# Encoder layer on one core: 27 instead of 24 in-projection pieces beside the first attention, 35 instead of 38 beside the second

## The chip, the cores and the metric

The kernel runs on one core of one Trainium2 chip, in a single launch. The metric is the device time of one execution in microseconds (us). The engines are named as the profile names them: PE (TensorE, matrix products; PEld is its weight load), DVE (VectorE), ACT (ScalarE), POOL (GpSimd), SP (SyncE, here the queue that issues nearly all DMAs). Every product is made of float32 values split into a high and a low part, as three matmuls (high x high, high x low, low x high).

## The reference

```python
# x (1, 2048, 1024) f32, one layer
h = rms_norm(x, norm_mix)
z = h @ w_in                      # q_A 512 | k_A 128 | v_A 128 | q_B 512 | k_B 512 | v_B 512 | gate_A 1024 | gate_B 1024
y_a = windowed_gqa(q_a, k_a, v_a, sink)      # 8 heads, 2 kv heads, |t-s| <= 128, ALiBi, sink logit
y_b = neighborhood_attn(q_b, k_b, v_b, rpb)  # 8 heads, 8 x 16 neighbourhood on the 32 x 64 grid
gates = sigmoid(concat(g_a, g_b) + b_gate)
merged = gates[:, :1024] * (y_a @ w_proj_a) + gates[:, 1024:] * (y_b @ w_proj_b)
x = x + merged @ w_out
x = x + square(relu(rms_norm(x, norm_mlp) @ w_up)) @ w_down
return rms_norm(x, norm_final)
```

## The kernel before

The 2048 tokens are four blocks of 512. The kernel goes through these stages, most of them one after another on PE:

1. The in-projection of blocks 0 and 1, by a scheme of seven products of half-size blocks (`in_quad`). Its results go to scratch tensors in HBM: `qs_a`, `ks_a`, `vs_a` for the first attention, `qs_b`, `ks_b`, `vs_b` for the second, `zg` for the gates.
2. The first attention (A): 32 units `attn_a(g, i)`, one for each of two key heads and 16 blocks of 128 queries. Beside it runs a part of the plain in-projection of blocks 2 and 3.
3. The second attention (B): 32 units `attn_b`, one for each of 8 heads and 4 column strips of the grid. Beside it runs another part of the plain in-projection.
4. What is left of the plain in-projection, then gates, projections, `w_out`, and the two products of the feed-forward part.

**A plain piece** is one 128-column tile of the in-projection for one block: `feature_tile` (L203 to L205), 8 x 3 matmuls of 128x512 into a PSUM bank `mm`, from the weight tile `whl` and the normalised input `hT`. There are 34 column tiles (`dense`: one of k_A, one of v_A, four of q_A, then k_B, q_B, v_B four times, then 16 of the gates), each for blocks 2 and 3, so 68 pieces. With each tile go its weight load on SP (L190), the split of the weights on ACT (L179) and POOL or DVE (L180), and with each piece its eviction and store. The generator `chain(dense)` hands them out one by one, in that order; each step loads the tile after next and splits the next.

**A unit of A** has, on PE, eight score matmuls `s` (L792), three groups of four transposes `pt` (L810, two PSUM banks) and six products `av` with the values (L815 with the high part, L816 with the low part of the transposed weights). DVE adds the bias and takes the maximum from PSUM (L794, four times), adds and inverts the sums (L800, L801), makes the low part of each transposed group (`pl`, L814) and adds the result's halves (L822). ACT takes the exponentials (L799, four times) and the high parts (`ph`, L813). POOL scales by the inverse sums (L803). A unit at the edge (i = 0 or 15) has two groups of transposes. **A unit of B** is built alike: scores L955, maximum L960, exponentials L966, transposes L983, high and low parts L988 and L989, products L995.

**The order** of the instructions on each engine is made when the program is built, by a scheduler that times the program and puts what is ready first; it follows the program's order in priority. `drive` lets the units of an attention go ahead of their second halves by two. `paced` then feeds the pieces in: piece n of a stage is held behind the last product of unit n x 32 // total - lag, so that the pieces are spread over the stage:

```python
def paced(filler, pieces, total, lag):
    for n in pieces:
        at = min(n * 32 // total - lag, 31)
        with tc.issue_after(done[at]) if at >= 0 else nullcontext():
            next(filler, None)
```

Here `done` is the list of the last products of the units of that attention (emptied between A and B), and `total` the number of pieces that the 32 units are to be spread over. For A the calls stand in two parts, one ahead of the later halves of the keys and values (`load_kv`), one behind; for B too, one after the first 15 units and one at the end, ahead of stage 4. `chain` is one generator, so a piece that A takes is one that B does not.

Of the kernel before, what the change touches and what calls it, by code (L numbers as in the profile page):

```python
# [95 lines left out]
def encoder_layer(ctx, tc, x, norm_mix, w_in, b_gate, sink, rpb, w_pa, w_pb, w_out,  # L96
# [77 lines left out]
    def flush(keep=0, queue=A):  # L174
        while len(pending) > keep:
            queue.dma_start(*pending.pop(0))
# [650 lines left out]
    def chain(gens):  # L827

        for k, g in enumerate(gens):
            if k + 2 < len(gens):  # L830
                next(gens[k + 2])
            if 0 < k < len(gens) - 1:
                next(gens[k + 1])
            yield from g

    def drive(units, live, last, ahead=2):

        for u in units:
            next(u)
            live.append(u)  # L840
            if len(live) > ahead:
                next(live.pop(0), None)
        while last and live:
            next(live.pop(0), None)
# [7 lines that stand above are left out]
# [26 lines left out]
    fill = chain(dense)  # L878
# [3 lines left out]
    for g in (1, 0):  # L882
        load_kv(g, 0)
    drive((attn_a(g, i) for g in (1, 0) for i in range(7)), live, False)
    paced(fill, range(12), 24, 3)
    flush(queue=SY)
    for g in range(2):
        load_kv(g, 1, began[8 + 3 * g])
    drive((attn_a(g, i) for g in range(2) for i in range(7, 16)), live, True)
    paced(fill, range(12, 24), 24, 3)  # L890
    del done[:]
    flush(queue=SY)
    s_a.close()
# [133 lines left out]

    units = ahead_of(all_b(), 1)
    drive((next(units) for _ in range(15)), live, False)
    paced(fill, range(20), 38, 4)  # L1030
    flush(queue=SY)
    drive(units, live, True)
    flush(queue=SY)
# [27 lines left out]

    first_y = load_y(0)
    first_load = last_dma[0]
    paced(fill, range(20, 44), 38, 4)
    s_h.close()


# [596 lines left out]
```

## Time and profile before

| | us |
|---|---|
| median of 3 runs | 2603.46 (2603.23 to 2605.39) |
| the profiled execution | 2603.09 |
| its span, first to last instruction | 2601.3 |
| first attention with its pieces, from the first score matmul to the first of B | 362.5 to 608.5 |
| second attention, to its last score matmuls | 608.5 to 978 |

The span is a little shorter than the execution's own time, which has what lies around the program too. Busy times of an engine are sums over its instructions. A matmul is drawn from its start to the end of its flow through the array, so that consecutive ones overlap in the drawing: the distance from one start to the next is what a matmul takes of PE. "Idle before" is the time in which the engine did nothing ahead of an instruction, with the instruction that released it.

### The profile page before, as it was taken

Reading aid. Unit: us, or ns where it says so; the run is one execution under the profiler, and the core shown is the slowest. Engines: PE = TensorE matmul, PEld = TensorE weight load, DVE = VectorE, ACT = ScalarE, POOL = GpSimd, SP = SyncE. Lnnn points to the kernel's source line nnn. Section 1 sums busy time; section 2 is a strip of 40 time slices with the busy share of each in tenths; the row PEclk is TensorE's granted clock in tenths of the full one; section 3 lists DMA queues with packets and bytes.
Section 4 is the critical chain, followed back from the end, with each engine's and each line's share of the span. In section 5 each row is a group of like instructions: output and inputs, shape, how many; then the busy total and the mean of one; then the engine's idle time right before and its main releaser. Section 6 shows DMA issues by size and latency. Waiting matters only on the chain.

```text
span 2601.3 us, 34630 instructions
## 1 busy us (share of the span) xinstructions
PE 2570.3 (99%) x12140; PEld 2143.2 (82%) x12140; DVE 1608.5 (62%) x2621; ACT 1232.9 (47%) x2261; POOL 366.8 (14%) x493
## 2 busy tenths in 40 slices
PE   8999999999999999999999999999999999999999
PEld 6888788788888888888888888888888888888887
DVE  8866666665544444665478667766656534554766
ACT  5334356665655555542335544644454322323454
POOL 1000124444645531000000000100000000000010
PEclk9999999999999999999999999999999999999999
DMA  5657485465976746865466665844428825444555
GB/s 186 203 154 207 135 260 160 121 170 154 244 211 180 205 137 189 270 205 160 144 195 213 232 227 202 307 167 149 155 102 314 288 97 186 146 149 167 186 191 173
DMA packets 354128, 490.40 MB, mean 189 GB/s; under 512 B 28809, under 2 KB 188809, under 8 KB 351777
## 3 DMA queue, kind: packets, MB, share of 16 engines
q1 hardware_dynamic: 346896, 471.14, 57.2%
q10 hardware_dynamic: 7056, 17.04, 1.8%
q8 instruction: 96, 1.57, 0.3%
q14 instruction: 80, 0.65, 0.1%
HBM read 328.64 MB, written 159.45 MB: 188 GB/s over the span
## 4 chain that ended last, share of the span: by engine, by line
PE 92%; DVE 3%; DMA 2%; ACT 2%; issue 1%; SPq 0%; POOL 0%; POOLq 0%; ACTq 0%; DVEq 0%
PE b L302 16%; PE b L304 16%; PE b L303 16%; PE mm L203 6%; PE mm L205 6%; PE mm L204 6%; PE zb L302 3%; PE zb L304 3%; PE zb L303 3%; PE pt L203 2%; PE pt L204 2%; PE pt L205 2%; PE av L995 2%; PE pt L983 2%; PE s L955 2%; PE pt L810 1%
## 5 line engine op out<-in xcount | busy, mean ns | idle before, releaser
L303 PE MATMUL b<-dwh,dah 128*128 128x512 f32 x896 | 348.5, 389 | 0.0
L304 PE MATMUL b<-dwh,dah 128*128 128x512 f32 x896 | 347.6, 389 | 0.0
L302 PE MATMUL b<-dwh,dah 128*128 128x512 f32 x896 | 339.6, 389 | 0.0
L298 ACT CAST dah<-da 128x1024 fp32r<-128x1024 f32 (+1 forms) x128 | 120.9, 945 | 367.9 <-PE b L304 245.4
L299 DVE TENSOR_TENSOR dah<-da,dah 128x1024 fp32r<-128x1024 f32 (+1 forms) x128 | 139.7, 1091 | 224.5 <-ACT dah L298 221.3
L303 PE MATMUL b<-ubh,uwhlb 128*128 128x512 f32 x592 | 230.3, 389 | 0.0
L302 PE MATMUL b<-ubh,uwhlb 128*128 128x512 f32 x592 | 230.2, 389 | 0.0
L304 PE MATMUL b<-ubh,uwhlb 128*128 128x512 f32 x592 | 229.2, 389 | 0.0
L203 PE MATMUL mm<-hT,whl 128*128 128x512 f32 x544 | 218.6, 402 | 0.0
L205 PE MATMUL mm<-hT,whl 128*128 128x512 f32 x544 | 215.3, 396 | 0.0
L204 PE MATMUL mm<-hT,whl 128*128 128x512 f32 x544 | 214.4, 394 | 0.0
L303 PEld LDWEIGHTS b<-dwh,dah 128*128 128x128 f32 x896 | 168.2, 188 | 35.0
L302 PEld LDWEIGHTS b<-dwh,dah 128*128 128x128 f32 x896 | 168.2, 188 | 34.9
L304 PEld LDWEIGHTS b<-dwh,dah 128*128 128x128 f32 x896 | 168.2, 188 | 34.9
L302 PE MATMUL zb<-zh,zwhl 128*128 128x512 f32 x476 | 186.0, 393 | 6.9 <-DVE st L242 2.0
L303 PE MATMUL zb<-zh,zwhl 128*128 128x512 f32 x476 | 185.8, 390 | 0.0
L304 PE MATMUL zb<-zh,zwhl 128*128 128x512 f32 x476 | 183.0, 390 | 1.8 <-DVE zwhl L299 1.8
L293 DVE TENSOR_TENSOR uc<-b,uc 128x512 f32<-128x512 f32 x160 | 109.2, 689 | 103.9 <-PE b L304 103.0
L1534 POOL TENSOR_TENSOR st<-st,power 128x1 f32<-128x1 f32 x16 | 13.3, 841 | 925.1 <-DVE st L1533 925.0
L302 PEld LDWEIGHTS b<-ubh,uwhlb 128*128 128x128 f32 x592 | 111.1, 188 | 23.5 <-issue 0.4
L303 PEld LDWEIGHTS b<-ubh,uwhlb 128*128 128x128 f32 x592 | 111.1, 188 | 23.1
L304 PEld LDWEIGHTS b<-ubh,uwhlb 128*128 128x128 f32 x592 | 111.1, 188 | 23.0
(255 smaller groups left out, 5842.2 us busy)
## 6 DMA issues: line engine op xcount, KB each, us to landing
at<-uc SPq DMA_DIRECT2D x224, 256.0 KB
da<-at SPq DMA_DIRECT2D x96, 512.0 KB
dw<-in_w_down_dram SPq DMA_DIRECT2D x160, 256.0 KB
uraw<-in_w_up_dram SPq DMA_DIRECT2D x32, 1024.0 KB
raw<-in_w_in_dram SPq DMA_DIRECT2D x34, 512.0 KB
zraw<-in_w_in_dram SPq DMA_DIRECT2D x16, 1024.0 KB
z<-zg SPq DMA_DIRECT2D x64, 256.0 KB
zg<-zc SPq DMA_DIRECT2D x32, 256.0 KB
```

What stands on the lines that cost most here:

```text
L203: PE.matmul(ps, lh, rh, start=first, stop=False)
L204: PE.matmul(ps, lh, rl, start=False, stop=False)
L205: PE.matmul(ps, ll, rh, start=False, stop=last)
L293: return eng.tensor_tensor(out=out, in0=a, in1=b, op=op).ins
L298: casts.append(A.copy(hi, src).ins)
L299: return eng.tensor_tensor(out=lo, in0=src, in1=hi.bitcast(F32), op=ALU.subtract).ins
L302: PE.matmul(ps, lh, rh, start=first, stop=False, skip_group_check=True)
L303: PE.matmul(ps, lh, rl, start=False, stop=False, skip_group_check=True)
L304: PE.matmul(ps, ll, rh, start=False, stop=last, skip_group_check=True)
L955: PE.matmul(ps[:, :n], q[:, i, :], kv[:, z, B_R0[i] // 4 : (B_R0[i] + B_NR[i]) // 4, 4 * B_C0[j] : 4 * (B_C0[j] + w)], start=z == 0, stop= ...
L983: PE.transpose(pt[:kp, at + (i - i0) * P : at + (i - i0 + 1) * P], s[i][:, rr : rr + kp], ident)
L995: last = PE.matmul(po[:, i0 * P : (i0 + ni) * P], v[:kp, c, :], src[:kp, o : o + ni * P], start=first, stop=(c == 7 and z == 1), skip_grou ...
```

## The change

The pieces beside A become 27 instead of 24: 13 in the first part, 14 in the second, spread as 27 over the 32 units, with the lag of 3 as before. Of B's pieces the first part becomes 18 instead of 20, the second 23 instead of 24, spread as 35 over the units instead of 38, with the lag of 4 as before. The three pieces that go over to A are both blocks of the third k_B tile and the first block of the third q_B tile.

```diff
@@ -882,12 +882,12 @@
     for g in (1, 0):
         load_kv(g, 0)
     drive((attn_a(g, i) for g in (1, 0) for i in range(7)), live, False)
-    paced(fill, range(12), 24, 3)
+    paced(fill, range(13), 27, 3)
     flush(queue=SY)
     for g in range(2):
         load_kv(g, 1, began[8 + 3 * g])
     drive((attn_a(g, i) for g in range(2) for i in range(7, 16)), live, True)
-    paced(fill, range(12, 24), 24, 3)
+    paced(fill, range(13, 27), 27, 3)
     del done[:]
     flush(queue=SY)
     s_a.close()
@@ -1027,7 +1027,7 @@
     units = ahead_of(all_b(), 1)
     drive((next(units) for _ in range(15)), live, False)
-    paced(fill, range(20), 38, 4)
+    paced(fill, range(18), 35, 4)
     flush(queue=SY)
     drive(units, live, True)
     flush(queue=SY)
@@ -1061,7 +1061,7 @@
     first_y = load_y(0)
     first_load = last_dma[0]
-    paced(fill, range(20, 44), 38, 4)
+    paced(fill, range(18, 41), 35, 4)
     s_h.close()
```

The order that this gives is built anew for every engine from the middle of A to the end of B.

## The prediction

> **What bounds the kernel now.** I read the page first, then the windows by stage, then PE's own groups and time line inside the first attention.
>
> ```profile
> span 2601.3 us, 34630 instructions
> PE 2570.3 (99%) x12140; PEld 2143.2 (82%) x12140; DVE 1608.5 (62%) x2621; ACT 1232.9 (47%) x2261; POOL 366.8 (14%) x493
> PEclk9999999999999999999999999999999999999999
> PE 92%; DVE 3%; DMA 2%; ACT 2%; issue 1%; SPq 0%; POOL 0%; POOLq 0%; ACTq 0%; DVEq 0%
> ```
>
> TensorE (PE) is the chain that ends last, at full granted clock throughout. The change leaves the number of its matmuls as it is: 68 plain pieces of 72 matmuls stand before and after, only at other places. So the time can move only through the time in which PE stands still between instructions. The windows by stage say where that is: first attention with its pieces (362.5 to 608.5), second attention (608.5 to 978), its last units and the pieces left over (to 1026).
>
> ```profile
> core 0: us, PE busy (x) PEld busy (x) DVE busy (x) ACT busy (x) POOL busy (x), PEclk, DMA share, GB/s
> 362.50:608.50 246.00, 240.40 (x1300) 199.93 (x1299) 152.16 (x448) 162.91 (x466) 110.70 (x173) 1.00 0.60 165
> 608.50:978.00 369.50, 368.95 (x2128) 322.81 (x2127) 179.20 (x456) 209.27 (x503) 191.92 (x213) 1.00 0.69 190
> 978.00:1026.00 48.00, 47.27 (x259) 40.15 (x259) 17.90 (x34) 25.36 (x48) 7.02 (x7) 1.00 0.46 131
> ```
>
> PE is idle 5.60 us in the first attention, 0.55 us in the second, though the second is half as long again. The donor stage is full and the receiving stage has holes. The holes are not spread evenly:
>
> ```profile
> 362.50:392.00 29.50, 28.75 (x158) 23.90 (x157) 17.63 (x66) 18.24 (x64) 13.46 (x24) 1.00 0.92 273
> 417.00:425.00 8.00, 7.50 (x48) 6.04 (x47) 6.49 (x18) 7.67 (x23) 5.08 (x7) 1.00 0.62 167
> 425.00:451.00 26.00, 26.00 (x141) 22.00 (x140) 15.06 (x44) 15.27 (x43) 10.47 (x17) 1.00 0.44 115
> 480.00:492.00 12.00, 9.91 (x61) 7.95 (x60) 9.00 (x27) 8.71 (x23) 5.64 (x8) 1.00 0.49 127
> 584.00:592.00 8.00, 7.63 (x45) 5.93 (x44) 5.43 (x18) 7.48 (x25) 5.57 (x8) 1.00 0.79 234
> ```
>
> Between two holes PE is 26.00 of 26.00 us busy; the holes come every 33 us or so, four units apart (32 units in 246 us, 7.7 us each). The pacing rule says why. Piece n of the first attention may start behind unit n*32//24 - 3, which for n = 3 to 23 gives 1,2,3, 5,6,7, 9,10,11, 13,14,15, 17,18,19, 21,22,23, 25,26,27: units 0, 4, 8, 12, 16, 20 and 24 free no piece, and there PE has attention alone.
>
> **What one hole costs.** The time line of PE from the last piece before one hole to the first piece behind it (start, length, line, tile, count):
>
> ```profile
> 584.19 0.39 PE L815 MATMUL av<-ph,va 128*128 128x512 f32 x1
> 584.42 0.69 PE L792 MATMUL s<-ka,qa 128*128 128x288 f32 x4
> 584.95 0.39 PE L816 MATMUL av<-pl,va 128*128 128x512 f32 x1
> 585.18 1.03 PE L810 MATMUL pt<-ident,sa 128*128 128x128 f32 x8
> 585.97 1.68 PE L792 MATMUL s<-ka,qa 128*128 128x288 f32 x6
> 587.64 0.50 PE L815 MATMUL av<-ph,va 128*128 128x512 f32 x1
> 587.99 0.39 PE L816 MATMUL av<-pl,va 128*128 128x512 f32 x1
> 588.22 0.83 PE L792 MATMUL s<-ka,qa 128*128 128x288 f32 x4
> 588.89 0.42 PE L815 MATMUL av<-ph,va 128*128 128x512 f32 x1
> 589.54 0.50 PE L816 MATMUL av<-pl,va 128*128 128x512 f32 x1 [0.23 <-DVE pl L814]
> 589.87 0.39 PE L815 MATMUL av<-ph,va 128*128 128x512 f32 x1
> 590.11 0.60 PE L810 MATMUL pt<-ident,sa 128*128 128x128 f32 x4
> 590.46 0.48 PE L816 MATMUL av<-pl,va 128*128 128x512 f32 x1
> 590.78 0.60 PE L810 MATMUL pt<-ident,sa 128*128 128x128 f32 x4
> 591.13 0.48 PE L203 MATMUL mm<-hT,whl 128*128 128x512 f32 x1
> ```
>
> The steps from start to start are PE's real prices: a 512-wide matmul 0.23 us (584.95 to 585.18), a 288-wide one 0.53/4 = 0.13 us (584.42 to 584.95), a transpose 0.11 us (590.11 to 590.78 holds four and one 512-wide matmul: (0.67 - 0.23)/4). From 584.19 to 591.13 stand 8 wide matmuls, 14 of 288 and 16 transposes: 1.84 + 1.86 + 1.76 = 5.46 us of work in 6.94 us. **The hole costs 1.5 us**, while the window shows only 8.00 - 7.63 = 0.37 us idle, since a matmul's drawn length (0.39) is longer than its step. [...] Priced by busy time alone, a hole would be worth 0.4 us and the whole change some 3 us.
>
> The same count over the whole stage checks the price:
>
> ```profile
> L203 PE MATMUL mm<-hT,whl 128*128 128x512 f32 x180 | 72.3, 401 | 0.0
> L810 PE MATMUL pt<-ident,sa 128*128 128x128 f32 x328 | 50.1, 272 | 2.5 <-DVE pl L814 2.3 <-DVE sta L801 0.2
> L792 PE MATMUL s<-ka,qa 128*128 128x288 f32 x224 | 46.3, 313 | 0.8 <-DVE sta L794 0.5
> L815 PE MATMUL av<-ph,va 128*128 128x512 f32 x80 | 33.3, 416 | 0.3 <-DVE ya L822 0.3
> L816 PE MATMUL av<-pl,va 128*128 128x512 f32 x80 | 33.3, 416 | 1.9 <-DVE pl L814 1.4
> ```
>
> L204 and L205 have 180 as well, so 700 wide matmuls x 0.23 = 161.0, 328 transposes x 0.11 = 36.1, 224 x 0.1325 = 29.7, and 48 small ones left of the 1300 at about 0.1 = 4.8: 231.6 us of work in 246, so 14.4 us lost (the rounding of 0.23 makes this good to 1.5 us either way). One part is a single accident, at 485.2 to 487.5:
>
> ```profile
> 486.29 0.16 DVE L800 TENSOR_TENSOR sta<-sta 128x4 f32<-128x4 f32 x1 [1.93 <-ACT sa L799]
> 486.76 0.69 DVE L814 TENSOR_TENSOR pl<-pt,ph 128x512 fp32r<-128x512 f32 x1
> 487.51 0.66 PE L810 MATMUL pt<-ident,sa 128*128 128x128 f32 x4 [2.02 <-DVE pl L814]
> ```
>
> VectorE (DVE) sits 1.93 us in L800, waiting for ScalarE's four exponentials of a later unit; the split L814 is queued behind it, and PE's next transposes wait for the PSUM bank that L814 frees: 2.02 us. The other 12.4 us over seven regular holes and one small one near 600 us are 1.55 us each, as counted above.
>
> The cause of a regular hole is VectorE. A unit needs of it four reductions, three splits and one addition:
>
> ```profile
> L814 DVE TENSOR_TENSOR pl<-pt,ph 128x512 fp32r<-128x512 f32 x81 | 55.3, 688 | 9.1 <-ACT ph L813 8.6
> L794 DVE CUSTOM_DVE_ANT_0 sa<-s,biasa,byhead 128x288 f32<-128x288 f32 x112 | 53.7, 513 | 32.5 <-PE s L792 18.1 <-PE pt L810 14.3
> L822 DVE TENSOR_TENSOR ya<-av,ya 64x512 f32<-64x512 f32 x27 | 18.4, 680 | 6.6 <-ACT ya L821 6.5
> ```
>
> 4 x 0.513 + 3 x 0.688 + 0.680 = 4.8 us, against PE's 8 x 0.13 + 12 x 0.11 + 6 x 0.23 = 3.7 us. Alone, a unit runs at VectorE's pace and PE loses about 1.1 us plus the latency of the first split; with a piece (24 x 0.23 = 5.5 us more on PE) PE is the slower of the two and loses nothing.
>
> **The change part by part.**
> *First attention, 24 to 27 pieces.* The gates become n*32//27 - 3 = 0,1,2, 4 to 8, 10 to 15, 17 to 21, 23 to 27: units 3, 9, 16 and 22 free no piece, and unit 0 now does. In the built program PE's order follows this: stretches without a piece lie between pieces 5 and 6, 10 and 11, 16 and 17, 21 and 22, where they lay between 2|3, 5|6, 8|9, 11|12, 14|15, 17|18 and 20|21; the one between 2 and 3 is cut in its middle. The stretch 10|11 has, instruction for instruction on PE, the order of the hole timed above, so it costs 1.5 us again. Six regular holes become four: -2 x 1.5 = **-3.0 us** (bounds -1.5 to -4). The accident's place gets a piece; in the new VectorE order the splits that a hole's transposes need stand ahead of that L800 in all four holes, or (16|17) one stands behind it with some 5 us of PE work between by the steps above. I take it as gone: **-2.0 us** (0 to -2.0). The hole at the start (0.75 us idle in 362.5:392, the largest of the regular ones) keeps its first half and has a piece in its second: **-1.3 us** (0 to -2.5).
>
> *What else a piece brings.* Each moved tile of two pieces brings a weight load and two stores per piece on SP's queue, one split on ScalarE and GpSimd, one eviction. In the first attention these engines have room (ACT 162.91, DVE 152.16, POOL 110.70 of 246 us, DMA share 0.60), PE waits there for no DMA, and keys, values and queries of the later half come out of earlier pieces than before, so their loads on SP start no later: 0.
>
> *Second attention, 38 to 35.* The rule n*32//35 - 4 still passes over every unit: each of the 32 frees at least one piece; only three of the six units that freed two lose the second one. A unit with one piece has 5.5 us of filler against the same 1 to 2 us of VectorE surplus. In its second half the kernel before already runs with about one piece per unit, and PE's idle time over the whole stage is 0.55 us. I take **+0.5 us** (0 to +4). The order on PE of the last units and of pieces 62 to 67 is the same, so the 0.73 us idle of 978 to 1026 stays.
>
> *Sum:* -3.0 - 2.0 - 1.3 + 0.5 = **-5.8 us**. The profiled execution took 2603.09 us (its span 2601.3 and 1.8 around it), so 2597.3; the median of the runs, 0.4 us above it, becomes **2597.7 us**. About 0.2% (5.2 us) is what a measurement of this kernel can tell from no change, so this stands just beyond that bound.
>
> **The rivals.**
> *The accident moves on (2600.6 us, chance 0.30).* VectorE's order is written anew, and one of the four holes, or the shortened start, has a split behind a waiting L800 after all: 2.0 us come back, and the start gives 0.4 instead of 1.3. -2.9 us. For it: it happened in one hole of seven. Against: the new order shows no such place without cover.
>
> *The holes close further (2594.9 us, chance 0.13).* With nine pieces in eight units less backlog is left at VectorE when a hole begins, and the four left cost 0.8 us instead of 1.5: 2.8 us more. Against: stretch 10|11 is the old order again.
>
> *The holes are a matter of buffers (2603.5 us, chance 0.05).* Two PSUM banks for transposes, not the missing piece, would make the bubble; then it moves with the units and nothing is gained. [...] The trace speaks against it as the whole cause: with the same two banks the windows with pieces show none (26.00 of 26.00).
>
> *Slower: the second attention starts to starve (2608.7 us, chance 0.07).* With one piece per unit, PE reaches the products av before ScalarE or VectorE has the halves of the transposes:
>
> ```profile
> 857.02 0.39 PE L995 MATMUL av<-phb,vb 128*128 128x256 f32 x1 [0.39 <-ACT phb L988]
> ```
>
> With 0.16 us hidden by the drawn length that is 0.55 us a time. In each of the 20-odd units that now have a single piece and had one or two before, this would be 20 x 0.55 = 11 us, less the first attention's 5.8: +5.2. It decides from about 11 such stalls for no gain at all (11 x 0.55 = 6), from 20 for slower by over 0.2%. Against: with half of the stage already at one piece per unit, its idle time is 0.55 us in all.
>
> **How the numbers follow.** The forecast has 0.45. Its own range, from the bounds of the two holes, the start and the second attention, is 2596 to 2599.5; about three parts in four of it lie beyond 0.2%. With the closing holes, faster by over 0.2% has 0.45 x 0.75 + 0.13 plus a little from milder forms of both, 0.52; slower by over 0.2% takes half of the starving case and some for what no row shows, 0.06; the rest, 0.42, is within 0.2%. The range for 8 in 10 reaches from the closing holes to the moved accident and a little beyond: 2594.5 to 2602.
>
> **What would show it.** Right: PE idle time of the first attention (5.60 us) falls to about 3; the waiting of transposes for L814 (2.3 us) is gone; holes stand at four places some 50 us apart; the first attention is longer by three pieces (3 x 5.5 = 16.6 us) less the gain, the second shorter by as much; PE idle in the second stays under 1.5 us. Wrong: a wait of about 2 us on L814 at a new place (the accident), or idle time of several us at L995 in the second attention (starving), or the same number of holes as before.

## The result, and the profile after

| | before | after |
|---|---|---|
| median of 10 runs, us | 2603.65 (2602.24 to 2605.80) | 2610.30 (2605.60 to 2613.91) |
| ratio, 95% interval | | 1.0024 (1.0016 to 1.0033) |
| the profiled execution, us | 2603.09 | 2611.57 |
| its span, us | 2601.3 | 2609.8 |
| mean granted TensorE clock in it | 1.000 | 0.998 |

The change makes the kernel slower by 6.6 us. The page of after (span; busy time of the engines):

```profile
span 2609.8 us, 34644 instructions
PE 2576.0 (99%) x12140; PEld 2143.9 (82%) x12140; DVE 1609.2 (62%) x2621; ACT 1232.7 (47%) x2261; POOL 366.3 (14%) x493
```

As many matmuls as before, a span 8.5 us longer. The windows of after by stage (first attention A; second attention B to its last score matmuls):

```profile
core 0: us, PE busy (x) PEld busy (x) DVE busy (x) ACT busy (x) POOL busy (x), PEclk, DMA share, GB/s
362.50:624.00 261.50, 256.06 (x1374) 214.12 (x1373) 156.06 (x451) 167.19 (x469) 113.08 (x174) 0.99 0.60 163
624.00:986.00 362.00, 358.49 (x2051) 309.18 (x2050) 176.08 (x453) 205.40 (x500) 189.16 (x212) 1.00 0.69 189
```

PE's idle time in A is 5.44 us (before 5.60; the prediction said about 3), in B 3.51 us (before 0.55; said under 1.5). As in the prediction, busy time hides most of it. So from here on a **stall** is counted from starts: the distance of two starts on PE less the price of the first instruction (0.227 us for 512 wide, 0.132 for 288, 0.110 for a transpose, others by width, an estimate from these), summed over a stage. B is taken to its last product (1015.4 before, 1023.7 after):

| stalls, us | before | after | difference | forecast |
|---|---|---|---|---|
| A | 16.9 | 16.2 | -0.7 | -6.3 |
| B | 12.3 | 21.6 | +9.3 | +0.5 |

The sum, +8.6, is the difference of the spans (8.5) within 0.1 us. The waits of PE in after that have to do with both attentions (engine, line, waited for: total, times, longest):

```profile
PE pt L810 <- DVE pl L814: 2.5, 1, 2.5
PE s L955 <- DMA kb<-ks_b: 2.2, 1, 2.2
PE s L955 <- DVE stb L960: 0.8, 4, 0.3
...
PE av L995 <- ACT phb L988: 0.2, 1, 0.2
```

Three things stand behind the two numbers.

**1. The accident moved.** The time lines of PE, DVE and ACT in A's first hole of after (start, length, and in brackets the idle time before and who ended it):

```profile
413.17 0.77 PE L792 MATMUL s<-ka,qa 128*128 128x288 f32 x4
416.44 0.66 PE L810 MATMUL pt<-ident,sa 128*128 128x128 f32 x4 [2.50 <-DVE pl L814]
417.03 0.75 PE L815 MATMUL av<-ph,va 128*128 128x512 f32 x1
417.58 0.63 PE L816 MATMUL av<-pl,va 128*128 128x512 f32 x1
418.01 0.63 PE L815 MATMUL av<-ph,va 128*128 128x512 f32 x1
```

```profile
413.80 0.16 DVE L800 TENSOR_TENSOR sta<-sta 128x4 f32<-128x4 f32 x1 [2.28 <-ACT sa L799]
...
414.27 0.69 DVE L449 SCALAR_TENSOR_TENSOR z<-mm,z 128x512 fp32r<-128x512 f32 x1
415.69 0.69 DVE L814 TENSOR_TENSOR pl<-pt,ph 128x512 fp32r<-128x512 f32 x1 [0.72 <-ACT ph L813]
```

```profile
413.67 0.57 ACT L448 ACTIVATE z<-mm 128x512 fp32r<-128x512 f32 x1
414.15 1.03 ACT L179 CAST whl<-raw 128x1024 fp32r<-128x1024 f32 x1
415.08 0.57 ACT L813 CAST ph<-pt 128x512 fp32r<-128x512 f32 x1
```

It is the picture of 485.2 before, at a new place: DVE sits 2.28 us in L800 waiting for exponentials, the split L814 is queued behind it, and PE's transposes wait for the bank that L814 frees. L800 is not what ends last, though, here or before. L814 also needs the high part that ACT makes (L813), and on ACT this stands behind the same exponentials. ACT before:

```profile
485.65 0.52 ACT L799 ACTIVATE sa<-sa,sta 128x288 f32<-128x288 f32 x1
...
486.17 0.56 ACT L813 CAST ph<-pt 128x512 fp32r<-128x512 f32 x1
```

Before, L813 ends at 486.73 and L814 starts at 486.76; in after L813 ends at 415.65 and L814 starts at 415.69. With L800 out of the way both would have waited until then. In after an eviction (L448) and a weight cast (L179) stand between the exponentials and L813 and put it off by 1.41 us (413.67 to 415.08); the stall is 2.50 us, not 2.02. And behind the stall matmuls start 0.43 us apart (417.58, 418.01) where 0.23 is the rule: the granted clock is 0.50 from 417.1 on, for 3.41 us.

**2. B waits for the keys of its second head.** PE and the DMA issues of SP in after:

```profile
676.92 0.38 PE L955 MATMUL s<-kb,qb 128*128 128x288 f32 x1
679.54 0.38 PE L955 MATMUL s<-kb,qb 128*128 128x288 f32 x1 [2.24 <-DMA kb<-ks_b]
679.75 0.46 PE L203 MATMUL mm<-hT,whl 128*128 128x512 f32 x1
680.01 0.63 PE L204 MATMUL mm<-hT,whl 128*128 128x512 f32 x1
680.44 0.63 PE L205 MATMUL mm<-hT,whl 128*128 128x512 f32 x1
```

```profile
663.44 0.37 SPq L190 DMA_DIRECT2D raw<-in_w_in_dram  x1
665.57 0.34 SPq L932 DMA_DIRECT2D kb<-ks_b  x1
...
667.13 2.29 SPq L731 DMA_DIRECT2D vs_b<-z  x2
```

The load is issued 5.7 us after A's last product (at 659.88), and its data are needed 11.3 us later. Before, it went out at 651.80 and was needed 10.6 us later, without a wait:

```profile
651.80 0.34 SPq L932 DMA_DIRECT2D kb<-ks_b  x1
```
```profile
662.44 0.42 PE L955 MATMUL s<-kb,qb 128*128 128x288 f32 x2
```

What differs to the eye is the traffic: a weight load 2.1 us ahead of it and two stores of v_B right behind, which belong to other tiles since the pieces moved. The mean busy share of the DMA engines is 0.99 between the issue and the need (666.0 to 679.5), against 0.95 before (652 to 663). No run tests which of these makes it late. Again half rate follows, seven matmuls 0.43 us apart at a granted clock of 0.50 (679.91 to 683.33). Together some 4 us.

**3. A stall of 0.4 to 0.9 us in about every second unit of B.** Between 690 and 990 there are 14 places with 7.5 us (before 5 with 2.2): +5.3 us. PE and ACT at one of them:

```profile
800.93 0.60 PE L983 MATMUL pt<-ident,sb 128*96 128x128 f32 x4
801.29 0.36 PE L995 MATMUL av<-phb,vb 96*128 96x256 f32 x1
...
802.31 0.49 PE L983 MATMUL pt<-ident,sb 128*96 128x128 f32 x3
802.56 0.51 PE L955 MATMUL s<-kb,qb 128*128 128x288 f32 x2
803.19 0.38 PE L995 MATMUL av<-phb,vb 96*128 96x256 f32 x1
803.49 1.10 PE L955 MATMUL s<-kb,qb 128*128 128x384 f32 x4
```

```profile
801.13 0.58 ACT L862 COPY z<-mm 128x512 f32<-128x512 f32 x1 [3.50 <-PE mm L205]
801.61 1.05 ACT L179 CAST whl<-raw 128x1024 fp32r<-128x1024 f32 x1
802.56 0.96 ACT L988 CAST phb<-pt 96x512 fp32r<-96x512 f32 x2
```

PE goes from the four transposes (800.93) straight to eight products of the group before (801.29 to 802.31), with no matmul of a piece between, and is ready for the product of the new group at 802.8, two 288-wide scores after 802.56; it starts at 803.19, since its high part L988 stands behind the weight cast. The place costs 0.92 us in all. The view of waits shows next to nothing of this (0.2, 0.3 us a time), since the drawn lengths cover it (the two scores from 802.56 are drawn 0.51 us long, for 0.26 us of work); only the starts do.

### The profile page after: what moved, and what is told of

Its sections match the earlier page's. It is cut to its first block, busy times and chain, and to the rows that moved or that the text cites. A ratio compares the mean times of both kernels' runs of the same rounds, so it can differ in the third digit from the quotient of the medians.

```text
span 2609.8 us, 34644 instructions
## 1 busy us (share of the span) xinstructions
PE 2576.0 (99%) x12140; PEld 2143.9 (82%) x12140; DVE 1609.2 (62%) x2621; ACT 1232.7 (47%) x2261; POOL 366.3 (14%) x493
## 4 chain that ended last, share of the span: by engine, by line
PE 90%; DVE 4%; DMA 2%; ACT 2%; issue 1%; SPq 0%; POOL 0%; POOLq 0%; DVEq 0%; ACTq 0%
PE b L302 15%; PE b L304 15%; PE b L303 15%; PE mm L203 6%; PE mm L205 6%; PE mm L204 6%; PE zb L302 3%; PE zb L304 3%; PE zb L303 3%; PE pt L203 2%; PE pt L204 2%; PE pt L205 2%; PE av L995 2%; PE s L955 2%; PE pt L983 2%; PE pt L810 1%
## 5 line engine op out<-in xcount | busy, mean ns | idle before, releaser
L302 PEld LDWEIGHTS b<-ubh,uwhlb 128*128 128x128 f32 x592 | 111.1, 188 | 23.5 <-issue 0.4
```

The costliest lines, as they stand in the source:

```text
L302: PE.matmul(ps, lh, rh, start=first, stop=False, skip_group_check=True)
```

## The experiments

The theories after the result: B loses because its units have one piece each (theory one of the first expectations), because of ScalarE's casts (theory one from x5 on), because of the order in which the pieces stand, or by the late keys alone. All runs are in one table: stalls of A and B, the recurring ones (places and us between 690 and 990), and **straight units**, counted in the built order of PE: units of the later two thirds of B in which PE goes from four transposes straight to eight products with no piece between. The last columns are medians and the ratio to the kernel before, run on the same chip. The stall columns come from one traced execution each, the medians from all: the traces of x12 and x14 are the fastest of their executions, that of x1 is the slowest, so a trace and a median can differ by several us.

| run | A | B | recurring | straight | median us | ratio (95%) |
|---|---|---|---|---|---|---|
| before | 16.9 | 12.3 | 5, 2.2 | 3 | 2603.65 | |
| after | 16.2 | 21.6 | 14, 7.5 | 11 | 2610.30 | 1.0024 (1.0016-1.0033) |
| x1 A 27, B spread as 38 | 14.7 | 21.8 | 7, 2.4 | 5 | 2616.18 | 1.0045 (1.0033-1.0058) |
| x2 A 24, B spread as 35 | 18.2 | 12.6 | 3, 1.5 | 5 | 2603.86 | 1.0001 (0.9992-1.0010) |
| x3 after, half the keys of head 1 | 16.8 | 18.6 | 15, 8.8 | 11 | 2608.24 | 1.0014 (1.0005-1.0023) |
| x4 after, A's lag 4 | 10.4 | 21.3 | 15, 10.3 | 11 | 2608.09 | 1.0018 (1.0008-1.0027) |
| x5 after, B's casts on DVE | 14.7 | 11.2 | 6, 2.4 | 5 | 2601.53 | 0.9987 (0.9978-0.9996) |
| x6 26 and 36 | 15.7 | 12.8 | 5, 2.5 | 6 | 2602.74 | 0.9992 (0.9984-1.0001) |
| x7 26 and 36, A's lag 4 | 12.3 | 14.2 | 5, 2.2 | 6 | 2603.62 | 0.9997 (0.9988-1.0005) |
| x8 before, A's lag 4 | 17.5 | 20.1 | 9, 3.5 | 4 | 2610.65 | 1.0020 (1.0011-1.0029) |
| x9 before, B's casts on DVE | 18.5 | 11.0 | 3, 1.0 | 2 | 2603.91 | 1.0000 (0.9991-1.0009) |
| x10 after, lag 4 and casts on DVE | 10.5 | 13.1 | 5, 2.8 | 5 | 2601.10 | 0.9988 (0.9979-0.9997) |
| x11 26 and 36, lag 4, casts on DVE | 12.3 | 11.7 | 4, 1.9 | 3 | 2598.25 | 0.9977 (0.9968-0.9986) |
| x12 25 and 37 | 12.1 | 14.5 | 11, 3.8 | 5 | 2605.74 | 1.0003 (0.9994-1.0012) |
| x13 after, half of each cast on DVE | 16.2 | 23.5 | 15, 8.4 | 11 | 2610.11 | 1.0025 (1.0015-1.0035) |
| x14 after, B's lag 5 | 16.5 | 12.0 | 2, 0.7 | 5 | 2608.18 | 1.0013 (1.0004-1.0021) |
| x15 after, B's lag 3 | 16.3 | 15.6 | 10, 6.1 | 4 | 2606.78 | 1.0015 (1.0006-1.0024) |
| x16 26 and 36, lags 4 and 5 | 12.2 | 16.8 | 5, 2.0 | 4 | 2604.68 | 1.0004 (0.9995-1.0012) |

The recurring column of x3, x4, x5, x10 and x13 holds one longer stall near 730 too (1.1 to 2.6 us, a late high part L988). x15's has the last products near 984 in it, with 2 us.

**Which half of the change costs (x1, x2).** Against after, and against before:

```diff
-    paced(fill, range(18), 35, 4)
+    paced(fill, range(18), 38, 4)
-    paced(fill, range(18, 41), 35, 4)
+    paced(fill, range(18, 41), 38, 4)
```
```diff
-    paced(fill, range(20), 38, 4)
+    paced(fill, range(18), 35, 4)
-    paced(fill, range(20, 44), 38, 4)
+    paced(fill, range(18, 44), 35, 4)
```

> First attention as after the change (27 pieces spread as 27), second attention with its 41 pieces spread as 38, as before the change. Theory one, the second attention pays: in the trace after the change it lost some 9 us more than before (about 4 us in one wait for the keys of head 1 and the half-clock time behind it, about 5 us in stalls of 0.3 to 0.9 us in nearly every unit that has one piece), while the first attention gained 0.5 us. Then the denser spread takes most of it back: 2601 to 2605 us. Theory two, the first attention pays: the accident that moved to the hole behind piece 5 (2.5 us idle, then matmuls at half speed) and whatever it shifts behind it is the loss; then this stays at 2608 to 2612 us. The wait for head 1's keys may stay in both.

> First attention as before the change (24 pieces), second attention with its 44 pieces spread as 35, one piece to a unit, the rest behind the last unit (the first part of its pieces is 18 instead of 20). Theory one (the second attention pays for one piece to a unit): 2608 to 2612 us, with stalls at the score matmuls and products of the second attention as after the change. Theory two (the first attention pays): 2602 to 2605 us, as before.

x2 gives B one piece per unit and loses nothing: one piece per unit is not the cost. (The keys of the second head come 1.0 us late there, with A as before, so a late load is not the mark of 27 pieces.) x1 has few recurring stalls, but its pieces run out (1024.7) before B's last products (1034.3), and 9.4 us of stalls lie behind B where after has 1.8; both theories put it too low.

**The late keys (x3).** Head 1 loads one copy of its keys (1 MB instead of 2) and uses it for both halves, so its scores are other numbers:

```diff
+        if h == 1: return k
...
-                          kv[:, z, B_R0[i] // 4 : (B_R0[i] + B_NR[i]) // 4, 4 * B_C0[j] : 4 * (B_C0[j] + w)],
+                          kv[:, z if h != 1 else 0, B_R0[i] // 4 : (B_R0[i] + B_NR[i]) // 4, 4 * B_C0[j] : 4 * (B_C0[j] + w)],
```

> The kernel after the change, but head 1 of the second attention loads only one of its two copies of the keys (1 MB instead of 2 MB) and uses that one twice: its scores are left wrong by that, its work on all engines is the same. If PE's wait of 2.2 us for these keys and the half-clock matmuls behind it are real losses, this is faster than after by some 4 us: 2605 to 2607 us, and the wait is gone from the trace. If the wait only stands where another would (the scores' banks or the splits late too), 2609 to 2611 us.

The wait is gone and with it the half rate behind it; B's stalls fall by 3.0 us, the median by 2.1. The wait is worth some 2 to 3 us of the 6.6, but the ratios of x3 and after overlap (1.0005 to 1.0023 against 1.0016 to 1.0033), so the medians alone do not show it.

**The accident (x4, x8).** A's lag is 4 instead of 3, in after and in before: `paced(fill, range(13), 27, 4)` and `paced(fill, range(12), 24, 4)`, the second parts alike.

> The kernel after the change with the first attention's lag 4 instead of 3: the pieces start one unit earlier, and in VectorE's order the split that the transposes of the hole behind piece 5 waited for no longer stands behind the reciprocal's wait; one such place with 3.7 us of PE work between stays. The second half of the second attention has the same order as after. If the accident and its half-clock time cost their 4 us, this is 2605 to 2608 us. If the first attention doesn't matter for the loss, 2609 to 2611 us.

> The kernel before with one thing else: the lag of the first attention is 4 instead of 3. If the lag alone takes the accident away: 2600 to 2601. If the accident depends on how many microseconds of PE work stand between the split that waits behind L800 and the transposes that need its bank (3.0 us here, as in the changed kernel, which had the accident): it stays, 2603 to 2605.

In x4 the accident is gone and A's stalls are 10.4 us, 6.5 less than before: the gain that was forecast (6.3), in the stage where it was forecast, though with a lag that the forecast did not have. Its median lies 2.2 us below that of after, with overlapping intervals; two waits in B, 1.2 us for queries and 2.4 us for a high part, take part of the gain. In x8 the accident comes up at the same hole as in after:

```profile
413.60 0.77 PE L792 MATMUL s<-ka,qa 128*128 128x288 f32 x4
416.88 0.66 PE L810 MATMUL pt<-ident,sa 128*128 128x128 f32 x4 [2.51 <-DVE pl L814]
```

For x4 and x8 that was foretold from the order alone: take the L814 that frees the bank, see whether it stands behind an L800, and count PE's work from the end of the scores that this L800 waits for to the transposes. By this count, with about 2.6 us of cover (before, x2) PE stood 2.0 us, with 3.0 (after, x8) 2.5; with 3.7 (x4) at most 0.7; with 4.3 (x6) the view has no such wait. The count needs no L800 to hold up the split: L813 waits for the same exponentials on ACT, and ends last. It does not size the stall, since what else stands in the queue (1.4 us on ACT in after) comes on top. x8's total was missed, since a load of queries came 3.4 us late in B.

**An even or an odd number (x6, x7, x12).** 26 pieces in A (`range(13), 26` and `range(13, 26), 26`), 42 in B (`range(18), 36`, `range(18, 42), 36`), with A's lag 3 and 4; then 25 and 43 (`range(12), 25`, `range(12, 25), 25`; `range(19), 37`, `range(19, 43), 37`).

> 26 pieces beside the first attention (13 and 13, spread as 26, lag 3), 42 beside the second (18 and 24, spread as 36, lag 4). An even number, so that a tile's two blocks fall on the same units of the second attention's order as with 24. Theory one (27, an odd number, shifts the tiles' weight loads and casts against the units): the recurring stalls of the second attention are 2 to 3 us as with 24, the built order shows a split behind a waiting L800 only with 4.3 us of PE work as cover, so no accident: 2598 to 2601. Theory two (every piece taken away from the second attention costs it, whatever its parity): two thirds of the changed kernel's 9.3 us there, 2605 to 2608.

> As the run with 26 and 36, with a lag of 4 instead of 3 in the first attention, so that each of its pieces is freed a unit earlier. The built order shows no split behind a waiting L800 with less than 5 us of PE work as cover, and fewest stretches in which PE goes straight from transposes to their products in the second attention (6, the changed kernel 11, the kernel before 4). Theory one: 6 us from the first attention, nothing lost in the second: 2597 to 2599. Theory two: 2604 to 2607.

> 25 pieces beside the first attention (12 and 13, spread as 25, lag 3), 43 beside the second (19 and 24, spread as 37), casts on ScalarE as before. An odd number again, one step from the kernel before. Theory one in its narrow form (an odd number sets the tiles' casts against the units): recurring stalls of 5 us or more in the second attention as with 27, 2605 to 2609. Its wide form (each split makes its own order, and the count of places where PE goes straight from transposes to products with a cast ahead of them decides; here 5, with 24 it was 4, with 26 10, with 27 11): 2 to 3 us of them, 2602 to 2605.

x6 costs B nothing (12.8): taking pieces away from B is not itself the cost. x12 shows that odd does not mean bad either (3.8 us). x7 lost 2 us to the late keys, and its median lies 4 us above its trace.

**The cast (x5, x9, x13).** x5 against after; x9 is the same edit of before:

```diff
-        A.copy(hl[:, 0], raw)
+        cast[0].tensor_copy(out=hl[:, 0], in_=raw) if cast[0] else A.copy(hl[:, 0], raw)
...
-    paced(fill, range(18), 35, 4)
+    cast[0] = V; paced(fill, range(18), 35, 4)
-    paced(fill, range(18, 41), 35, 4)
+    paced(fill, range(18, 41), 35, 4); cast[0] = None
```

In x13 the cast line shares the work (and `cast[0]` is set as in x5):

```diff
+        (A.copy(hl[:, 0, 0:4], raw[:, 0:4]), cast[0].tensor_copy(out=hl[:, 0, 4:8], in_=raw[:, 4:8])) if cast[0] else A.copy(hl[:, 0], raw)
```

> The changed kernel with one thing else: in the second attention the high part of the plain pieces' weights (L179) is made by VectorE instead of ScalarE; the first attention has the same order as in the changed kernel. Theory one (in the second attention ScalarE does a cast of 1.05 us directly ahead of the high parts L988 that PE is about to need, and these are the 14 recurring stalls): the recurring stalls between 690 and 990 fall from 7.5 us to 3 or less, the first attention and the wait for the keys stay, 2605 to 2607. Theory two (the stalls come from one piece per unit at these places, the cast only happens to stand there): they stay near 7 us, 2609 to 2612.

> The kernel before (24 and 38) with one thing else: the cast L179 of the second attention's pieces on VectorE. Theory one (the cast is what the changed kernel's second attention loses by, because 27 pieces put it ahead of the high parts that PE needs; with 24 it stands there in few units): little to win here, the 5 recurring stalls of 2.2 us halve: 2601 to 2603. Rival (the cast costs the second attention about as much with any split, and its removal from ScalarE is a gain of its own of some 9 us, which says nothing of the change): 2594 to 2597.

> The changed kernel with one thing else: of each cast of the second attention's pieces ScalarE makes the first half (128x512) where it made the whole, VectorE the second half at the same time. PE's order in the second attention stays as in the changed kernel but for some forty instructions that move by a place; the 11 stretches in which PE goes straight from transposes to products are the same 11. If the 1.05 us of the cast ahead of the high parts make the recurring stalls: about half a microsecond less of each that has the cast ahead of it, so that 7.5 us between 690 and 990 become 3 to 4.5: 2604 to 2607. If the order of PE makes them (straight from transposes to products, whatever ScalarE does), and moving the whole cast helped because it also changed that order: still 7 us or more, 2609 to 2611.

x5 gives back 8.8 us by the medians, and x9 nothing: so far the cast theory has all it asked for. But x5 also has another order on PE (5 straight units instead of 11), and the late keys come in time in it, which is some 4 us of its gain. x13 keeps the order, and there the theory fails that the length of the cast alone makes the stalls. PE, ACT and DVE at the same place as above:

```profile
806.51 0.51 PE L955 MATMUL s<-kb,qb 128*128 128x288 f32 x2
806.85 0.28 PE L995 MATMUL av<-phb,vb 96*128 96x256 f32 x1
807.43 1.10 PE L955 MATMUL s<-kb,qb 128*128 128x384 f32 x4 [0.30 <-DVE stb L960]
```
```profile
805.57 0.62 ACT L179 CAST whl<-raw 128x512 fp32r<-128x512 f32 x1
806.08 1.18 ACT L988 CAST phb<-pt 96x512 fp32r<-96x512 f32 x2
```
```profile
806.68 0.69 DVE L960 CUSTOM_DVE_ANT_0 sb<-s,biasl 128x512 f32<-128x512 f32 x1 [0.56 <-PE pt L983]
807.30 0.08 DVE L960 DVE_READ_ACCUMULATOR2_ANT stb<- 128x1 f32 x1
```

The high parts come in time now (the product starts at 806.85, with no gap), and PE stops one instruction later: the next scores wait for a PSUM bank that DVE's L960 frees. The stall is 0.92 us, as in after. Two chains end close together, and mending one shows the other; what both lack is PE work in front.

**The order alone (x14, x15, x16, and a second trace of x14).** Casts on ScalarE, only lags changed: `range(18), 35, 5` and `range(18, 41), 35, 5` in after, the same with 3, and 26 and 36 with A's lag 4 and B's lag 5.

> The changed kernel with one number else: the lag of the second attention's pieces is 5 instead of 4, so that each of them is freed a unit earlier; the casts stay on ScalarE, 27 and 35 pieces. The built order has 5 units from the seventh on in which PE goes straight from the transposes to the products with no piece between (the changed kernel 11, the kernel before 3, the run with the cast on VectorE 5). If this order makes the recurring stalls: they fall from 7.5 us to 2 to 3.5 between 690 and 990, the accident in the first attention stays: 2602 to 2606. If the casts on ScalarE or the number 35 make them: 6 us or more, 2608 to 2611.

> The changed kernel with the lag of the second attention's pieces at 3 instead of 4; casts on ScalarE, 27 and 35 pieces. 4 units in which PE goes straight from the transposes to the products. If this order makes the recurring stalls: 2 to 3.5 us between 690 and 990, 2602 to 2606. Otherwise 6 us or more, 2608 to 2611.

> 26 and 36 pieces, lag 4 in the first attention, lag 5 in the second, casts on ScalarE: pacing numbers alone are changed against the kernel before. The built order shows no split that waits behind L800 with little cover in the first attention, and 4 units without a piece between transposes and products in the second. 12 us of stalls in the first attention, 11 to 13 in the second: 2598 to 2602; with a late load of the second head's keys as with lag 4 in both (2.1 us) 2601 to 2604.

> The same kernel as the run with lag 5 in the second attention, for a second trace: its first profiled execution was the fastest of its 12 (2602.9 us, their median 2608.2). If the longer executions have the recurring stalls that the first trace lacked: over 5 us of them between 690 and 990. If they differ by waits for DMA or by the clock behind a long stall: the recurring stalls stay under 2 us, and the rest shows as a wait for keys or queries of 2 us or more or as matmuls of 0.43 us instead of 0.23.

x14 at the place that answers to the one above:

```profile
797.92 0.60 PE L983 MATMUL pt<-ident,sb 128*96 128x128 f32 x4
798.27 0.48 PE L203 MATMUL mm<-hT,whl 128*128 128x512 f32 x1
...
800.79 0.28 PE L995 MATMUL av<-phb,vb 96*128 96x256 f32 x1
...
801.98 0.38 PE L955 MATMUL s<-kb,qb 128*128 128x288 f32 x1
802.20 0.28 PE L995 MATMUL av<-phb,vb 96*128 96x256 f32 x1
```

Between transposes and products (798.27 to 800.79) stand nine matmuls of the piece and two scores, and the product at 802.20 comes 4.3 us after the transposes instead of 2.3, without a stall. The recurring stalls are 0.7 us (7.5 in after), in both traces, with the cast on ScalarE and 27 and 35 pieces as they were: **the place of the pieces in PE's order makes them**. x15 is a miss: it has 4 straight units and 6.1 us, so the count of straight units is a rough sign only; x3, x4 and x13 have it at 11 because their order in B is nearly that of after.

The traces show what sets the costly places apart. From 690 us to B's last score matmul, all 19 traces together have 117 straight units. In 60 of them no weight cast (L179) starts in the 2 us from the transposes on: 55 of these lose at most 0.27 us in the next 4.2 us, by the distances of starts, and in 51 PE takes two scores and then four products of the new group in a row. In 39 a whole cast on ACT starts there: 38 lose 0.58 to 1.05 us, and in all 38 PE takes two or four scores, then one product, then more scores. The other five of the 60, which lose 0.8 us, have that order too. With the whole cast on DVE 10 of 11 lose at most 0.26 us. In x13, with half a cast and the order of after, six of seven still lose 0.73 to 1.04 us. Before has 3 straight units, none with a cast; after has 11, 7 of them with one. So a straight unit costs when the cast falls into it, and the lost time goes with the order that the builder then writes. That the builder puts the scores ahead because it times the cast there is my reading; no run tests it.

The median of x14 fell by 2.1 us only, and its interval overlaps that of after (1.0004 to 1.0021 against 1.0016 to 1.0033); the late keys are gone in it too. Its second trace shows where the rest went: behind B, a wait for a weight cast, with half rate behind it (0.43 us from 1039.69 to 1040.12).

```profile
1036.71 0.39 PE L205 MATMUL s<-page,whl 128*128 128x512 f32 x1
1039.02 0.50 PE L203 MATMUL mm<-page,whl 128*128 128x512 f32 x1 [1.92 <-ACT whl L179]
...
1039.69 0.63 PE L203 MATMUL s<-page,whl 128*128 128x512 f32 x1
1040.12 0.63 PE L204 MATMUL s<-page,whl 128*128 128x512 f32 x1
```

The first trace, the fastest of its 12 executions, has this wait with 0.8 us. x16 has it too (1.15 us), and the late keys (2.6 us).

**Put together (x10, x11).** x10 is after with x4's and x5's edits, x11 is x7 with x5's.

> The changed kernel with both disputed parts mended: lag 4 in the first attention (with which the accident was gone and its stalls were 10.4 us instead of 16.2) and the cast of the second attention's pieces on VectorE (with which its stalls were 11.2 us instead of 21.6). If the two losses are separate and add up: 2610.3 less 9 less 5: 2595 to 2598. If the order between the two attentions brings a late load back (keys or queries of the next head), as it did with lag 4 alone: 2598 to 2602.

> 26 and 36 pieces, lag 4 in the first attention, cast on VectorE in the second. The first attention as in the run with 26 and lag 4 (12.3 us of stalls), the second without the 2.2 us of recurring stalls; the wait of 2.1 us for the keys of the second head may stay. If it stays: 2600 to 2602; if the new order ends it: 2596 to 2599.

x10 loses 1.6 us to a late load of queries at 668, and 1.5 at a high part near 727. x11, with 24.0 us of stalls in both attentions against 29.2 before, is faster than both kernels: 2598.25 us, 0.9977 (0.9968 to 0.9986).

## Why the prediction was wrong, point by point

*What bounds the kernel, and what a hole costs:* right. The time moved through PE's stalls alone, and counted from starts they add up to the change of the span within 0.1 us. A's forecast of -6.3 is reached in x4, with another lag: -6.5.

*Six holes become four, -3.0:* wrong for after. Outside the start and the accident's hole, the larger places of A have 8.4 us of stalls before (1.5, 1.2, 1.55, 1.7, 1.6 and 0.8 near 600) and 8.1 after (1.6 near 468, 2.4 from 478 to 494, 2.8 from 530 to 546, 1.3 near 585). Fewer stretches without a piece, but two of them have come apart into two stalls each. I priced them by the one stretch (10|11) that looked as before. In x4 the four cost 1.3 to 1.9 us each, and the start 0.55.

*The accident is gone, -2.0:* this step failed outright. I wrote that the splits a hole's transposes need stand ahead of the waiting L800 in all four holes. In the hole 5|6 they do not; the order had it on show, and 3.0 us of cover is not enough. I also read only VectorE's queue: in the accident before, too, the split waited last for ScalarE's high part (486.73), which stands behind the same exponentials there. The rival "the accident moves on" was right (0.30), at 2.50 us and some 1 us of half rate, where it had 2.0.

*The start, -1.3:* right in kind; the stalls there went from 2.75 to 0.76 us, -2.0.

*What else a piece brings, 0, and loads that start no later:* right for A's own keys, wrong for B's. I looked at the loads inside A and not at the border, where the issue of B's second keys (L932) waits 1.7 us for the store of A's last result (3.2 us before) and goes out among loads and stores of other tiles. Some 4 us in the trace, 2 us by x3.

*Second attention, +0.5 (0 to +4):* the step that decided, +9.3. The price was drawn from how many pieces a unit has; x2 says that number is harmless. What counts is whether the piece lies between the transposes and their products, and whether a weight cast falls into a unit where it does not; three pieces moved shift that for every unit behind. The recurring stalls are +5.3 us of the +9.3 and the late keys nearly all the rest. The rival "B starves" had the place (L995 and what follows), twice the size (11 us against 5.3), and a mechanism, one piece per unit, that x2 refutes; that its total (2608.7) came near is luck. It got 0.07.

*The range:* the bounds of the four terms, added, give 2595 to 2606 for the median, where the prediction's own range was 2596 to 2599.5, and its range for 8 in 10 was 2594.5 to 2602. The measured 2610.3 lies outside all three, and B's term, +9.3 against a bound of +4, is the one that was mis-sized most.

*The rivals as cases:* I gave chances to single mishaps, and two came together: the accident's +2.9 and B's loss. The forecast for the profiled execution, 2597.3 us, plus what A did not give (5.6) and what B took beyond the forecast (8.8), makes 2611.7; it took 2611.57.

## What to carry to other kernels

Where a scheduler writes the order anew, a change of three pieces in 68 is a change of every wait behind them: read the built order for queues behind a waiting instruction, on every engine that feeds the place, and count the bottleneck engine's work that covers them (here 4.3 us were enough and 3.0 were not), before pricing what the edit was about. Count stalls by the distances of starts; the busy time and the view of waits showed less than half of these. When taking away a late releaser leaves the stall as long (0.92 us in after and in x13), look for another one that ended close behind it; what helped here was work in front of both (x14: 0.7 us of recurring stalls instead of 7.5).

## What the runs showed of the hardware

In these traces half rate of PE (512-wide matmuls 0.427 us apart instead of 0.227) stands behind stalls of 1.70 us and more, and the same stall has it in one execution and not in the next. All kernels here have a stall of 1.70 to 1.74 us at 50 us, in a part that none of them changed; six to eight matmuls 0.427 us apart follow it in 8 of 19 traces (x1, x2, x5, x6, x7, x11, x13 and the second of x14), and none in the other 11. The granted clock is 0.50 for 3.41 us each time. Of the stalls of 2.4 us and more, half rate follows those at 413 (2.66 us) and 677 (2.49 us) in after, and none the one of 2.72 us in x16. What decides which stall has it is not shown. Within a trace the starts of the half-rate spells lie whole multiples of their own length in the clock record, 3.413 us, apart (417.1 and 679.9 in after: 77 of them; 54.4, 679.0 and 1030.6 in x1: 183 and 103); no run shows why. A spell costs about 1.5 us on top of the wait: behind the late keys of after, eight matmuls take 3.39 us (680.01 to 683.40) where 8 x 0.227 = 1.82 us is their price. After, with two such spells in its trace where that of before has none behind a stall, also scatters more (2605.6 to 2613.9, before 2602.2 to 2605.8); no run tests whether the one makes the other. The runs of before that were made beside the experiments have a median of 2602.5 us where the mean clock was 1.000 (19 runs) and of 2604.6 where it was 0.998 (34 runs).
